# Moving 61 gathered dot products into a later part of a mixture kernel, and splitting a gate multiplication over two engines

## The chip, the cores and the metric

The kernel runs on one NeuronCore of a Trainium2 chip. The metric is device time in microseconds, the median of several runs: 3538.58 us before the change (three runs, 3538.36 to 3540.56). The engines are called TensorE (PE in the profile), VectorE (DVE), ScalarE (ACT), GpSimd (POOL) and SyncE (SP); each works through its own queue in program order.

## The reference

The program is two transformer-like blocks one after the other. Only the feed-forward of the first block, `peer_ffn`, matters here. For each of 512 tokens and 8 heads it picks 16 of 16384 experts and sums them:

```python
s1, s2 = q1 @ sub_keys_1, q2 @ sub_keys_2          # 128 scores each, per head
v1, i1 = top_k(s1, 16); v2, i2 = top_k(s2, 16)
cand = v1[:, None] + v2[None, :]                   # 16 x 16 sums
top_s, pos = top_k(cand, 16)
expert = i1 * 128 + i2 at pos                      # 16 of 128 x 128 experts
gate = softmax(top_s)
act = gelu(x . w_down[expert]) * gate              # 128 dot products a token
y = sum(act * w_up[expert])                        # 128 rows a token
```

`w_down` and `w_up` have 16384 rows of 1024 floats each (64 MB).

## The kernel before, in words

The function `phase_b` computes this in two ways at once. For the last 384 tokens (`ND` = 3 tiles of 128) it is done densely: all 128 blocks of 128 experts are scored for all tokens, the Gelu of the scores is multiplied with a gate map that is zero where a token did not choose an expert, and the product is multiplied with all of `w_up`. For the first 128 tokens (`NG` = 1 tile) the chosen rows are gathered from memory.

**Parts in time.** The code of `phase_b` is scheduled by hand: instructions stand in each engine's queue in the order in which Python issues them. There are three loops over expert blocks `b`:

1. *Score blocks*, `b` from 0 to `FUSE` - 1 = 87. `score` (L1206) takes a prepared weight, runs 24 matmuls of 128x384 into a bank `pS`, and ScalarE writes the Gelu into a stage `sst`, which goes out to memory (`smap`) every second block. Beside it runs the generator `side`: first `topk` for four tiles (VectorE: top-16 searches, comparisons, sums, a softmax whose exponential is on ScalarE at L911), then `gate_map` (L918) for three tiles.
2. *Fused blocks*, `b` from `FUSE` to 127: `score`, then `act` (L1203: VectorE multiplies score and gate into `ua`, ScalarE copies its rounded high part `uah`, VectorE subtracts for the low part `ual`), then `up_mm` for the block before: 18 matmuls of 128x512 into six banks `py`.
3. *Up blocks*, `b` from 0 to `FUSE` - 1: scores come back from `smap`, `act`, `up_mm`.

**Weights.** Each block of weights (128x1024 floats) is loaded by SP three ahead, and split two ahead (`split`, L1342): ScalarE casts the high part `wsh` (L1346), GpSimd subtracts for the low part `wsl` (L1347). A fused block needs two such splits, the others one.

**Gate maps.** `gate_map` makes, for four tokens at a time, one-hot rows of the two expert indices (L944, 128x1024, both in one comparison), multiplies the first half with the gates (L946, 128x512), and in the next step `flush` lets TensorE multiply the two one-hots (L932, bank `pgm`) and ScalarE copy the result into a stage `gst` (L933); every fourth step the stage goes to memory (`gmap`). The one-hots have two buffers, so the comparison of a step waits for the matmuls of the step two before. There are 32 steps a tile, 96 in all.

**Gathers.** `gather_tiles` (L953) has 128 down rows and 64 pairs of up rows to fetch. GpSimd issues an indirect DMA (L974) seven ahead into eight buffers; VectorE forms the dot product of a down row with the token (L984, 128x1024); up pairs are multiplied on TensorE (L1008).

**Budgets.** How much of a generator is issued in a block is set by `take(gen, budget)`: each `yield` of the generator names a cost, and steps are issued while credit is left. A top-k tile costs 35 credits, a gate-map step 1.9, a dot product 1, an up pair 2. `side` gets 3.3 a block for the first 12 blocks and `SR` after; `gat` gets `GR` in score blocks from block 12 on, `GF` in fused blocks, `GR2` in up blocks:

```python
if up is None and take(side, 3.3 if b < 12 else SR):   # L1228
    sr.close(); up = self.pool(sr, "up", side="right")
if up is not None and FUSE // 8 not in GT and b > FUSE - 8:
    load_g(FUSE // 8)                                  # on SP's queue, ahead of later weights
if b >= 12:
    take(gat, GR)
```

When `side` is done its pool is released, the pool `up` takes its room, and the first gate map is loaded back from memory.

Of the kernel before, what the change touches and what calls it, by code (L numbers as in the profile page):

```python
# [12 lines left out]
AF = mybir.ActivationFunctionType  # L13
# [78 lines left out]
    return {k: np.ascontiguousarray(v) for k, v in o.items()}  # L92


SR, GR, GR2 = 4.0, 0.8, 1.4
FUSE, GF = 88, 2.0
NG, GB = 1, 8
ND = 4 - NG
NT = 128 * ND
# [7 lines left out]
class K:  # L107
# [810 lines left out]
    def gate_map(self, pool, t, e2, gate):  # L918
        nc = self.nc
        pT = pool.tile([128, 3, 128], F32, name="gmT", bufs=1)  # L920
        p = self.bank("pgt")
        for q, src in enumerate((e2[:, 0], e2[:, 1], gate)):
            nc.tensor.transpose(p[:, q * 128:(q + 1) * 128], src.rearrange("p h k -> p (h k)"), self.ident)
        nc.scalar.copy(pT, p[:, :384].rearrange("p (q t) -> p q t", q=3))
        yield 0.0
        pend = None

        def flush(last):
            stage, q, b, oh = pend
            p = self.bank("pgm")  # L930
            for w in range(4):
                nc.tensor.matmul(p[:, w * 128:(w + 1) * 128], oh[:, 1, w], oh[:, 0, w], start=True, stop=True)  # L932
            nc.scalar.copy(stage[:, :, 4 * q:4 * q + 4].rearrange("p i t -> p t i"),  # L933
                           p.rearrange("p (t i) -> p t i", t=4))
            if q == 3:
                nc.scalar.dma_start(self.gmap[(t - NG) * 8 + b], stage.rearrange("p i t -> p (i t)"))

        for b in range(8):
            stage = pool.tile([128, 128, 16], F32, name="gst", bufs=2)
            for q in range(4):  # L940
                oh = pool.tile([128, 2, 4, 128], F32, name="oh", bufs=2)
                t0 = b * 16 + q * 4
                B4 = [128, 2, 4, 128]
                nc.vector.tensor_tensor(oh, self.io128[:, None, None, :].to_broadcast(B4),  # L944
                                        pT[:, :2, t0:t0 + 4][:, :, :, None].to_broadcast(B4), op=OP.is_equal)
                nc.vector.tensor_mul(oh[:, 0], oh[:, 0], pT[:, 2, t0:t0 + 4][:, :, None].to_broadcast([128, 4, 128]))  # L946
                yield 1.9
                if pend is not None:
                    flush(False)
                pend = (stage, q, b, oh)  # L950
        flush(True)
# [1501 lines left out]
```

## Time and profile before

| what | value |
|---|---|
| median of the runs | 3538.58 us |
| the profiled execution's own time | 3550.41 us |
| its span, first to last instruction | 3548.7 us |
| mean granted TensorE clock | 0.939 |
| busy: TensorE, VectorE, ScalarE, GpSimd | 3163.8, 2415.0, 1328.9, 1808.1 us |
| first and last score activation of `phase_b` | 677.0 and 1596.3 us |

The profiled execution is some 12 us longer than the median. A row of a timeline gives the start in us, the duration in us, the engine, the line, the operation, the tile written and the tiles read, and in brackets how long the engine stood idle before and what released it. A row of a grouping gives a count, the busy time in us and the mean in ns. Reported durations contain time in which an instruction has begun and is held back.

### The profile page before, as it was taken

Reading aid. Unit: us, or ns where it says so; the run is one execution under the profiler, and the core shown is the slowest. Engines: PE = TensorE matmul, PEld = TensorE weight load, DVE = VectorE, ACT = ScalarE, POOL = GpSimd, SP = SyncE. Lnnn points to the kernel's source line nnn. Section 1 sums busy time; section 2 is a strip of 40 time slices with the busy share of each in tenths; the row PEclk is TensorE's granted clock in tenths of the full one; section 3 lists DMA queues with packets and bytes.
Section 4 is the critical chain, followed back from the end, with each engine's and each line's share of the span. In section 5 each row is a group of like instructions: output and inputs, shape, how many; then the busy total and the mean of one; then the engine's idle time right before and its main releaser. Section 6 shows DMA issues by size and latency. Waiting matters only on the chain. (4 is left out here: it accounts for less than half of the span.)

```text
span 3548.7 us, 43925 instructions
## 1 busy us (share of the span) xinstructions
PE 3163.8 (89%) x16324; PEld 2429.7 (68%) x16324; DVE 2415.0 (68%) x3200; ACT 1328.9 (37%) x1887; POOL 1808.1 (51%) x970
## 2 busy tenths in 40 slices
PE   7777899978788899999999999877899999999995
PEld 7767798977788899876666686754455555555541
DVE  6999756999999779836666664676555455554524
ACT  3234523332455433323232334253344434444421
POOL 4656553466555489977777643233233323333313
PEclk8888899989999999999999998889999999999997
DMA  3111122355666688779989721568999999999996
GB/s 100 60 60 60 34 66 87 111 199 192 215 242 234 226 272 284 266 240 328 328 316 335 251 95 49 179 230 311 341 371 380 390 388 376 389 394 382 380 387 238
DMA packets 286347, 868.15 MB, mean 245 GB/s; under 512 B 21232, under 2 KB 82064, under 8 KB 282928
## 3 DMA queue, kind: packets, MB, share of 16 engines
q1 hardware_dynamic: 232496, 666.64, 52.3%
q0 software_dynamic: 43264, 155.02, 12.3%
q10 hardware_dynamic: 10368, 43.63, 3.2%
q8 instruction: 130, 2.13, 0.2%
q14 instruction: 89, 0.73, 0.1%
HBM read 805.89 MB, written 59.32 MB: 244 GB/s over the span
## 5 line engine op out<-in xcount | busy, mean ns | idle before, releaser
L1347 POOL TENSOR_TENSOR wsl<-wf,wsh 128x1024 fp32r<-128x1024 f32 x272 | 687.4, 2534 | 415.4 <-ACT wsh L1346 413.5
L1799 DVE TENSOR_TENSOR m_wl<-m_wf,m_wh 128x1024 fp32r<-128x1024 f32 x256 | 395.6, 1570 | 467.6 <-ACT m_wh L1797 452.8
L1799 POOL TENSOR_TENSOR m_wl<-m_wf,m_wh 128x1024 fp32r<-128x1024 f32 x128 | 326.3, 2556 | 695.7 <-ACT m_wh L1797 600.3
L1797 ACT CAST m_wh<-m_wf 128x1024 fp32r<-128x1024 f32 x384 | 383.4, 1047 | 379.0 <-issue 161.1
L1347 DVE TENSOR_TENSOR ual<-ua,uah 128x384 fp32r<-128x384 f32 x128 | 386.4, 3019 | 168.0 <-ACT uah L1346 168.0
L1346 ACT CAST wsh<-wf 128x1024 fp32r<-128x1024 f32 x272 | 285.4, 1051 | 363.1 <-POOL wsl L1347 166.9
L2202 PE MATMUL pd<-m_wf,m_xs 128*64 128x512 f32 x1632 | 393.5, 630 | 1.6 <-DMA m_wf<-in_e_down_dram 1.6
L126 PE MATMUL pS<-xh,wsl 128*128 128x384 f32 x1024 | 352.6, 344 | 25.2 <-POOL wsl L1347 25.2
L124 PE MATMUL pS<-xh,wsh 128*128 128x384 f32 x1024 | 356.8, 348 | 16.8 <-ACT wsh L1346 16.8
L125 PE MATMUL pS<-xl,wsh 128*128 128x384 f32 x1024 | 350.9, 343 | 0.0
L125 PE MATMUL pd<-m_wl,m_xh 128*128 128x512 f32 x768 | 307.3, 400 | 13.5 <-DVE m_wl L1799 13.5
L124 PE MATMUL pd<-m_wh,m_xh 128*128 128x512 f32 x768 | 314.6, 410 | 0.0
L124 PE MATMUL py<-wsh,uah 128*128 128x512 f32 x768 | 308.9, 402 | 1.0 <-ACT uah L1346 1.0
L126 PE MATMUL py<-wsh,ual 128*128 128x512 f32 x768 | 303.9, 396 | 3.1 <-DVE ual L1347 3.1
L126 PE MATMUL pd<-m_wh,m_xl 128*128 128x512 f32 x768 | 306.5, 399 | 0.0
L125 PE MATMUL py<-wsl,uah 128*128 128x512 f32 x768 | 303.5, 395 | 0.0
L2202 PEld LDWEIGHTS pd<-m_wf,m_xs 128*64 128x64 f32 x1632 | 115.0, 143 | 225.8 <-issue 214.1
L377 DVE SCALAR_TENSOR_TENSOR cvo<-glu,cv,cvo 128x512 f32<-128x512 f32 x200 | 223.6, 1158 | 1.2
L126 PEld LDWEIGHTS pS<-xh,wsl 128*128 128x128 f32 x1024 | 196.7, 192 | 30.7 <-POOL wsl L1347 29.4
L124 PEld LDWEIGHTS pS<-xh,wsh 128*128 128x128 f32 x1024 | 197.9, 193 | 25.0 <-ACT wsh L1346 17.7
L984 DVE SCALAR_TENSOR_TENSOR gu<-gu,xn 128x1024 f32<-128x1024 f32 x128 | 207.2, 1639 | 5.4 <-DMA gu<-in_w_dn_dram,idx 5.4
L974 POOL DMA_INDIRECT gu<-in_w_dn_dram,idx x128 | 182.5, 1426 | 50.2 <-DVE gu L984 28.9
(612 smaller groups left out, 6586.0 us busy)
## 6 DMA issues: line engine op xcount, KB each, us to landing
m_wf<-in_e_gate_dram SPq DMA_DIRECT2D x132, 1024.0 KB, 11.7
m_wf<-in_e_up_dram SPq DMA_DIRECT2D x132, 1024.0 KB, 11.2
m_wf<-in_e_down_dram SPq DMA_DIRECT2D x132, 1024.0 KB, 11.8
wf<-in_w_dT_dram SPq DMA_DIRECT2D x128, 512.0 KB, 4.2
wf<-in_w_up_dram SPq DMA_DIRECT2D x128, 512.0 KB, 5.6
gmap<-gst ACTq DMA_DIRECT2D x24, 1024.0 KB, 6.2
G<-gmap SPq DMA_DIRECT2D x16, 1536.0 KB, 13.3
smap<-sst ACTq DMA_DIRECT2D x44, 384.0 KB, 3.5
```

What stands on the lines that cost most here:

```text
L124: nc.tensor.matmul(ps, a[0], b[0], start=start, stop=False)
L125: nc.tensor.matmul(ps, a[0], b[1], start=False, stop=False)
L126: nc.tensor.matmul(ps, a[1], b[0], start=False, stop=stop)
L377: nc.vector.scalar_tensor_tensor(acc, glu[:, 16 + q:528 + q], self.cv[:, o + q:o + q + 1], acc, op0=OP.mult, op1=OP.add)
L974: nc.gpsimd.indirect_dma_start(out=u, out_offset=None, in_=todo[issued][0], in_offset=bass.IndirectOffsetOnAxis(ap=todo[issued][1], axis=0))
L984: nc.vector.scalar_tensor_tensor(us[0], us[0], 1.0, xn, op0=OP.mult, op1=OP.mult, accum_out=act[i][:, j:j + 1])
L1346: nc.scalar.copy(hi, src)
L1347: (lo_eng or nc.vector).tensor_tensor(lo, src, hi, op=OP.subtract)
L1797: nc.scalar.copy(wh[:, k2], w[:, k2])
L1799: eng.tensor_tensor(wl[:, k2], w[:, k2], wh[:, k2], op=OP.subtract)
L2202: nc.tensor.matmul(ps[0][c], x[:, k], wh[:, k2, ns], start=(k == 0), stop=False)
```

## The change

Three constants move and one VectorE operation is split. The gathered dot products get no budget in score blocks (`GR` 0.8 to 0.0) and more in fused and up blocks (`GF` 2.0 to 3.0, `GR2` 1.4 to 1.45). The top-k and gate-map generator gets 4.5 credits a block instead of 4.0. Fused blocks begin at 80 instead of 88. In the gate maps, VectorE multiplies the gates in for two of the four tokens, and ScalarE for the other two, as an Identity activation with a scale per partition, in place.

```diff
-SR, GR, GR2 = 4.0, 0.8, 1.4
-FUSE, GF = 88, 2.0
+SR, GR, GR2 = 4.5, 0.0, 1.45
+FUSE, GF = 80, 3.0
...
                 nc.vector.tensor_tensor(oh, self.io128[:, None, None, :].to_broadcast(B4),
                                         pT[:, :2, t0:t0 + 4][:, :, :, None].to_broadcast(B4), op=OP.is_equal)
-                nc.vector.tensor_mul(oh[:, 0], oh[:, 0], pT[:, 2, t0:t0 + 4][:, :, None].to_broadcast([128, 4, 128]))
+                nc.vector.tensor_mul(oh[:, 0, :2], oh[:, 0, :2], pT[:, 2, t0:t0 + 2][:, :, None].to_broadcast([128, 2, 128]))
+                for w in range(2, 4):
+                    nc.scalar.activation(oh[:, 0, w], oh[:, 0, w], AF.Identity, scale=pT[:, 2, t0 + w:t0 + w + 1])
                 yield 1.9
                 if pend is not None:
                     flush(False)
```

## Rows read from the trace of the kernel before

**Rows 1.** The page's first part: busy time, share of the span, instructions.

```profile
PE 3163.8 (89%) x16324; PEld 2429.7 (68%) x16324; DVE 2415.0 (68%) x3200; ACT 1328.9 (37%) x1887; POOL 1808.1 (51%) x970
```

**Rows 2.** Busy us by window: stretch, length, PE, PEld, DVE, ACT, POOL, clock, DMA.

```profile
672.00:893.90 221.90, 177.94 (x947) 173.93 (x945) 208.57 (x427) 69.78 (x91) 139.83 (x65) 0.91 0.55 184
893.90:1214.20 320.30, 284.37 (x1813) 277.45 (x1814) 300.81 (x260) 161.56 (x186) 177.41 (x82) 0.97 0.67 234
...
1251.70:1596.80 345.10, 336.45 (x1694) 296.79 (x1694) 261.68 (x215) 117.96 (x159) 299.40 (x156) 0.99 0.79 264
1596.80:2053.00 456.20, 446.71 (x2088) 311.71 (x2087) 300.57 (x216) 139.77 (x195) 329.31 (x201) 0.99 0.86 303
```

**Rows 3.** ScalarE's timeline: score activations, start and duration in us.

```profile
855.82 0.49 ACT L1212 ACTIVATE sst<-pS 128x384 f32<-128x384 f32 x1 [2.24 <-PE pS L126]
...
860.06 0.49 ACT L1212 ACTIVATE sst<-pS 128x384 f32<-128x384 f32 x1 [2.81 <-PE pS L126]
...
1014.13 0.49 ACT L1212 ACTIVATE sst<-pS 128x384 f32<-128x384 f32 x1 [2.22 <-PE pS L126]
...
1020.16 0.49 ACT L1212 ACTIVATE sst<-pS 128x384 f32<-128x384 f32 x1 [1.65 <-PE pS L126]
1020.68 0.33 ACTq L1227 DMA_DIRECT2D smap<-sst  x1
...
1548.87 0.49 ACT L1212 ACTIVATE sst<-pS 128x384 f32<-128x384 f32 x1 [7.17 <-PE pS L126]
...
1558.35 0.49 ACT L1212 ACTIVATE sst<-pS 128x384 f32<-128x384 f32 x1 [4.27 <-PE pS L126]
```

**Rows 4.** VectorE's timeline in the fused part, one block.

```profile
1303.79 4.97 DVE L1347 TENSOR_TENSOR ual<-ua,uah 128x384 fp32r<-128x384 f32 x1 [0.58 <-ACT uah L1346]
1308.69 1.21 DVE L984 SCALAR_TENSOR_TENSOR gu<-gu,xn 128x1024 f32<-128x1024 f32 x1
...
1309.84 1.21 DVE L984 SCALAR_TENSOR_TENSOR gu<-gu,xn 128x1024 f32<-128x1024 f32 x1
...
1310.98 0.55 DVE L1200 TENSOR_TENSOR ua<-sst,G 128x384 f32<-128x384 f32 x1
1312.11 4.97 DVE L1347 TENSOR_TENSOR ual<-ua,uah 128x384 fp32r<-128x384 f32 x1 [0.58 <-ACT uah L1346]
```

**Rows 5.** GpSimd's timeline beside it.

```profile
1303.56 4.78 POOL L1347 TENSOR_TENSOR wsl<-wf,wsh 128x1024 fp32r<-128x1024 f32 x2
1308.50 1.10 POOL L974 DMA_INDIRECT gu<-in_w_dn_dram,idx  x1 [0.16 <-issue]
1309.91 1.96 POOL L974 DMA_INDIRECT gu<-in_w_dn_dram,idx  x1 [0.30 <-DVE gu L984]
```

**Rows 6.** GpSimd's timeline where the gathers begin: two of seven issues.

```profile
739.13 0.94 POOL L974 DMA_INDIRECT gu<-in_w_dn_dram,idx  x1 [0.30 <-issue]
740.37 0.94 POOL L974 DMA_INDIRECT gu<-in_w_dn_dram,idx  x1 [0.30 <-issue]
```

**Rows 7.** The dot products' line alone (L984), by window; a read of the accumulator each.

```profile
672.00:893.90 221.90, 51.59 (x42) 0.91 0.55 184
```

**Rows 8.** ScalarE's timeline: the last of four top-k exponentials.

```profile
890.81 0.31 ACT L911 ACTIVATE gate<-gate 128x128 f32<-128x128 f32 x1 [16.24 <-DVE gate L910]
```

**Rows 9.** The gate multiplication: its group from 893 to 1221 us, one unhindered.

```profile
L946 DVE TENSOR_TENSOR oh<-oh,gmT 128x512 f32<-128x512 f32 x96 | 136.8, 1425 | 3.3
...
1007.96 0.69 DVE L946 TENSOR_TENSOR oh<-oh,gmT 128x512 f32<-128x512 f32 x1
```

**Rows 10.** ScalarE's groups from 672 to 2060 us, shapes apart.

```profile
L933 ACT COPY gst<-pgm 128x512 f32<-128x512 f32 x96 | 100.9, 1071 | 63.2 <-PE pgm L932 62.8 <-ACT gst L933 0.5
...
L993 ACT COPY aT<-pgt 128x128 f32<-128x128 f32 x1 | 0.3, 266 | 0.9 <-PE pgt L991 0.9
```

**Rows 11.** All instructions of L1448, an Identity activation after L1488's Gelu.

```profile
L1448 ACT ACTIVATE c_qT<-pq,c_bq x5: 688/690/690, 2103.3 to 2125.1; 128x512 f32<-128x512 f32 x5
```

**Rows 12.** ScalarE's timeline after the last gate map.

```profile
1237.35 1.04 ACT L1346 CAST wsh<-wf 128x1024 fp32r<-128x1024 f32 x1 [11.88 <-DMA wf<-in_w_dT_dram]
```

## The prediction, as it was made before the result was known

> **What bounds the kernel now.** I read the page's busy shares first [rows 1], then the windows by part [rows 2], then the timelines of single engines inside the parts. The reader sees in [rows 1] that TensorE is busy for 89% of the span, so VectorE's work only counts where TensorE waits for it. [rows 2] shows where. In the first two parts (top-k, then gate maps) VectorE is busy 209 of 222 us and 301 of 320 us; in the fused part (scores and up products together) and in the up part TensorE is busy 336 of 345 us and 447 of 456 us. So the first 542 us are VectorE's, and everything from 1251.7 us on is TensorE's.
>
> TensorE's own pace comes from consecutive score activations [rows 3]. A bare score block takes 4.24 us (860.06 less 855.82). A block with two gate-map steps and no dot product takes 6.03 us (1020.16 less 1014.13), so one step's matmuls cost (6.03 - 4.24) / 2 = 0.90 us. A fused block takes 8.32 us (VectorE's `ual` comes at 1303.79 and 1312.11, [rows 4]), of which the up product is 8.32 - 4.24 = 4.08 us. With one gathered up pair it takes 9.48 us (1558.35 less 1548.87), so a pair is 1.16 us.
>
> The rows to look at longest are VectorE's in the fused part [rows 4] beside GpSimd's [rows 5]. The two hold each other out: `ual`, a 0.55 us subtraction, lasts 4.97 us, because GpSimd's two weight subtractions (4.78 us together) run in that time. GpSimd's loop is full as well: 0.16 gap + 1.10 first gather issue + 0.30 gap + 1.96 second issue + 4.78 = 8.30 us. The second issue ends 0.82 us after the dot product it lay beside (1309.84 + 1.21 = 1311.05, end 1311.87); with VectorE waiting an issue takes 0.94 us, 1.24 us from the next [rows 6]. So at two dot products a block three engines stand at 8.3 us, and VectorE and GpSimd have nothing left.
>
> **The change part by part.**
>
> *The order of the work, counted from the budgets.* The top-k and gate-map generators cost 140 + 182.4 credits. Before, the gate maps run from block 37 to 82; after, with 4.5 a block, from 34 to 74, with 4.5 / 1.9 = 2.37 steps a block instead of 2.11. Before, 61 of the 128 dot products fall into the first part and 67 into the fused part, two a block. After, none falls into the first part and all 128 into the fused part, three a block: 42.7 of its 48 blocks. There are 8 fewer score-only blocks, 8 more fused ones, 8 fewer up-only ones. TensorE's total work stays as it was; only its waiting changes.
>
> *Top-k part (35 blocks after, 38 before).* VectorE is busy 208.6 us [rows 2], 51.6 us of it in dot products [rows 7], of which 21 x 1.21 = 25 us is their work and 26 us waiting for GpSimd. ScalarE stands behind VectorE here (16.24 us at one exponential, [rows 8], four such places), which holds weight casts back. Without the dot products VectorE needs 157 us, and it was idle for 13. If all their waiting goes, the part takes 157 (TensorE's floor, 35 x 4.24 = 148, lies under it); if the waiting merely falls on other two-input operations, 222 - 27 = 195. I take 175, nearer the first, since most top-k operations that remain keep their usual duration beside the weight subtraction: -47 us.
>
> *Gate maps.* The multiply of 128x512 had a mean of 1.43 us, but 0.69 unhindered [rows 9]; half of it is about 0.35. Two ScalarE multiplications of 128x128 come in its place: the trace has 0.27 for a copy of that shape [rows 10] and 0.31 for an exponential [rows 8], so about 0.6 us a step, 55 us of ScalarE in all. ScalarE has the room (162 of 320 us busy), but not the place: the multiplications of a step stand in its queue behind the block's Gelu (0.49 us) and, every second block, the store's issue (0.33 us, [rows 3]). TensorE wants that step's one-hots 0.90 us after the scores end; ScalarE delivers them at about 0.04 + 0.49 + 0.6 = 1.1, or 1.5 with the issue. That is a new wait of about 0.5 us, and in a block with three steps, where the third multiplication also stands behind a 1.07 us eviction [rows 10], about 1.3. Behind it wait the evictions, the weight cast, and GpSimd's subtraction for it. TensorE's floor is 40.3 x 4.24 + 96 x 0.90 = 257 us; the waits add 25.4 x 0.5 + 14.9 x 1.3 = 32, the stray stalls of such a part 6. I take 295, with bounds 262 (no new wait) and 310: -25 us. Identity should cost no table: five activations with it follow a tanh-Gelu without a load [rows 11]. Were there loads after all, they would lie in ScalarE's queue at the same place, which rival D prices.
>
> *The stretch from the last gate map to the fused part.* It holds five blocks in both kernels and the same hole (ScalarE waits 11.88 us for weights, [rows 12], whose loads stand in SP's queue behind the gate map's load, which waits for the released pool): 37.5 us, unchanged.
>
> *Fused part.* The gathers start only here, so seven issues go out at once, 6 x 1.24 + 0.94 = 8.4 us of GpSimd ahead of a weight subtraction; with two weights prepared ahead I put 4 us of that on TensorE (0 to 8). Then three dot products a block. At the least, if VectorE and GpSimd only keep each other's tensor operations out, a block needs 3 x 1.15 (their spacing in [rows 4]) + 0.55 + 0.55 + 4.78 = 9.33 us. VectorE's loop as it stands, with one dot product more, is 8.32 + 1.15 = 9.47. GpSimd's loop with a third issue is 8.30 + 0.30 + 0.94 = 9.54, or 10.56 if that issue too is held by a dot product for 1.96. I take 10.0, between these, and keep 9.3 and 10.6. Total: 4 + 42.7 x 10.0 + 5.3 x 8.32 + 8 pairs x 1.16 + 7 for the turn from dot products to up rows (ScalarE waits 7.17 us for the scores that end before 1548.87, [rows 3]) = 491; before 345: +146 us. Gathers themselves have room: DMA is busy 79% here [rows 2], and a longer block lowers it.
>
> *Up part.* 8 x 4.08 + 1.16 less: -34 us. The slightly larger budget moves nothing: all pairs are issued inside it in both kernels.
>
> *Sum.* -47 - 25 + 146 - 34 = +40 us against the profiled execution's span of 3548.7 (3550.4 with what lies around it). That execution is 12 us above the median of the runs, so the forecast for the median is 3538.6 + 40 = 3579.
>
> *A rule of the Trainium skill.* The 1.96 us issue beside a dot product [rows 5] against 0.94 alone [rows 6] says that a two-input VectorE operation holds a gather issue back. The Trainium skill, "SBUF — State Buffer", section "Who interferes with whom", has it otherwise: such an operation contends with what GpSimd reads, not with its descriptor generation (which the page marks as inferred). By the rows a block is 10.0 and the sum +40; by the page issues stay short, and the lock on the tensor operations alone is left, which is rival B.
>
> **The rivals.**
>
> *B: only the tensor operations exclude each other; gather issues are not held.* GpSimd's loop is then 4.78 + 0.16 + 3 x 0.94 + 0.60 = 8.36, VectorE and GpSimd together 9.33, fused part 463 us: +12, 3551 us. For it: a first issue takes 1.10 although a dot product starts in it. Against it: the steady 1.96 of every second issue.
>
> *C, not slower: the whole of VectorE's relief reaches TensorE.* Place: the first two parts. ScalarE's multiplications arrive in time (VectorE, freed, runs a step ahead), and the exponentials no longer find VectorE behind. The parts go to 157 and 262 us, -65 and -58: with the fused part as forecast that is -123 + 146 - 34 = -11, 3528 us; with rival B's fused part -39, 3500. It decides from the point where the first two parts together give 112 us. For it: VectorE's 94% in both. Against it: ScalarE's in-order queue, and that TensorE waits in the gate maps now only 320 - 45 x 4.24 - 96 x 0.90 = 43 us.
>
> *D: worse.* The third issue always held and a wait added by it (10.6), ScalarE's place costing more (310), the top-k waits staying (195): -27 - 10 + 172 - 34 = +101, 3640 us.
>
> That the change does not do what it says can be set aside: with a budget of 0.0 no credit comes up before block 80.
>
> **How the numbers follow.** Forecast 0.50, B 0.15, C 0.22, D 0.13. The bounds for faster and slower are 0.2%, 7 us. The forecast gives 0.03 faster, 0.02 same, 0.45 slower; B 0.03, 0.03, 0.09; C 0.18, 0.03, 0.01; D all slower. Together faster 0.24, same 0.08, slower 0.68. The forecast's own range is 3549 (9.3 a block) to 3604 (10.6). The whole range takes in B, more than half of C and a part of D: 3510 to 3625.
>
> **What would show it.** Right: dot products only after block 80, three a block; score activations there 9.5 to 10.6 us apart, TensorE waiting for `wsl` in that part; issues of nearly 2 us, three a block; the first part shorter by some 70 us, with `pgm` waiting for ScalarE's `oh`. Wrong: fused blocks under 9.1 us (the sum changes sign there: 40 / 42.7 = 0.9 less than forecast), a dot product running while a weight subtraction runs, gate-map blocks near 6.4 us, or table loads beside Identity.

## The result, and the profile after

The changed kernel takes 3586.71 us (median of 4 runs, 3583.53 to 3588.86); on the same chip the kernel before takes 3539.57 (3538.36 to 3542.55). The ratio is 1.0131, interval 1.0114 to 1.0149: slower, near the forecast of 3579. The profiled execution has a span of 3586.8 us and took 3588.56, so it lies 1.9 us above its median, while the one of before (3550.41) lies 10.8 above the 3539.57; the spans differ by 38.1 us and the medians by 47.1.

The page's busy shares of the changed kernel, for [rows 1]:

```profile
PE 3179.2 (89%) x16324; PEld 2443.5 (68%) x16324; DVE 2359.2 (66%) x3200; ACT 1386.6 (39%) x2079; POOL 1786.5 (50%) x970
```

They hardly moved. VectorE works 56 us less and ScalarE 58 us more, and the kernel is slower: the page's first part can't say where. The windows by part, in the columns of [rows 2], can:

```profile
666.40:842.60 176.20, 159.74 (x875) 158.10 (x873) 169.02 (x381) 64.04 (x84) 103.05 (x35) 0.95 0.43 143
842.60:1157.00 314.40, 271.52 (x1698) 268.75 (x1699) 194.54 (x194) 212.86 (x369) 97.42 (x40) 0.93 0.47 164
...
1190.50:1664.30 473.80, 415.42 (x2038) 360.01 (x2038) 389.53 (x353) 142.05 (x192) 416.37 (x241) 0.98 0.87 287
```

In the first part VectorE still fills 169 of 176 us, but there is less of it. In the gate maps VectorE fell from 301 to 195 us busy and the stretch became only 6 us shorter: nobody is full there now, so something waits. In the fused part TensorE, 98% busy before, is busy 415 of 474 us.

The same cuts in both kernels, by the starts of the first one-hot comparison (L944), the last, the last score activation ahead of the fused blocks, and the last of all (us; the last columns are experiments told below):

| part | before | changed | difference | forecast | e3 | e6 | e10 |
|---|---|---|---|---|---|---|---|
| start to first scores | 677.0 | 671.4 | -5.6 | 0 | 672.7 | 672.8 | 667.7 |
| top-k | 217.8 | 172.1 | -45.6 | -47 | 171.9 | 172.4 | 171.9 |
| gate maps | 321.4 | 312.8 | -8.6 | -25 | 252.8 | 312.7 | 253.0 |
| to the fused part | 35.1 | 33.7 | -1.4 | 0 | 40.9 | 33.7 | 41.0 |
| fused part | 345.1 | 473.8 | +128.7 | +146 | 481.2 | 406.4 | 409.2 |
| up part and the rest | 1952.4 | 1923.0 | -29.4 | -34 | 1922.1 | 1919.1 | 1919.4 |
| span | 3548.7 | 3586.8 | +38.1 | +40 | 3541.6 | 3517.1 | 3462.1 |

The signs are as forecast; the gate maps gave a third of what was put on them. The first row varies between 667.7 and 677.0 us among the kernels of this case, although none of the edits touches that stretch, so a few us in one row of one profile show nothing.

**The fused block.** VectorE's timeline in the changed kernel, for [rows 4] (start, duration, instruction, idle time ahead of it):

```profile
1315.70 4.95 DVE L1349 TENSOR_TENSOR ual<-ua,uah 128x384 fp32r<-128x384 f32 x1 [0.58 <-ACT uah L1348]
1320.57 1.21 DVE L986 SCALAR_TENSOR_TENSOR gu<-gu,xn 128x1024 f32<-128x1024 f32 x1
...
1321.72 1.22 DVE L986 SCALAR_TENSOR_TENSOR gu<-gu,xn 128x1024 f32<-128x1024 f32 x1
...
1324.01 0.62 DVE L1202 TENSOR_TENSOR ua<-sst,G 128x384 f32<-128x384 f32 x1
1325.21 4.96 DVE L1349 TENSOR_TENSOR ual<-ua,uah 128x384 fp32r<-128x384 f32 x1 [0.58 <-ACT uah L1348]
```

GpSimd's beside it, for [rows 5]:

```profile
1315.47 4.75 POOL L1349 TENSOR_TENSOR wsl<-wf,wsh 128x1024 fp32r<-128x1024 f32 x2
1320.38 1.10 POOL L976 DMA_INDIRECT gu<-in_w_dn_dram,idx  x1 [0.16 <-issue]
1321.79 1.95 POOL L976 DMA_INDIRECT gu<-in_w_dn_dram,idx  x1 [0.30 <-issue]
1324.04 0.94 POOL L976 DMA_INDIRECT gu<-in_w_dn_dram,idx  x1 [0.30 <-issue]
1325.00 4.74 POOL L1349 TENSOR_TENSOR wsl<-wf,wsh 128x1024 fp32r<-128x1024 f32 x2
```

And TensorE's wait for the low part of a weight, with two score activations of ScalarE, for [rows 3]:

```profile
1312.54 0.49 ACT L1214 ACTIVATE sst<-pS 128x384 f32<-128x384 f32 x1 [4.55 <-PE pS L126]
1317.93 0.44 PE L126 MATMUL pS<-xh,wsl 128*128 128x384 f32 x1 [0.95 <-POOL wsl L1349]
1322.08 0.49 ACT L1214 ACTIVATE sst<-pS 128x384 f32<-128x384 f32 x1 [4.32 <-PE pS L126]
```

From weight subtraction to weight subtraction GpSimd takes 1325.00 - 1315.47 = 9.53 us, and the score activations follow at 9.54. GpSimd has no gaps here but those of 0.16 and 0.30 us ahead of its issues, so its loop is the block. One issue in three is held to 1.95 us; the third runs in 0.94, because VectorE is then at the short `ua`. In 16 of 128 cases that one is held too, to 1.32, until 0.8 us after `ua`, and the block takes 9.9. Over blocks 84 to 121 the mean is (1593.49 - 1236.14) / 37 = 9.66 us. By the view of waits from 1236 to 1593 us, TensorE and its weight load stand here:

```profile
PEld pS L126 <- POOL wsl L1349: 51.9, 37, 1.7
...
PE pS L126 <- POOL wsl L1349: 40.1, 37, 1.4
```

One wait a block, and 51.9 / 37 = 1.40 us is what the block has grown by (9.66 less 8.28, TensorE's own pace, which e6 shows below). (The weight load waits along with TensorE; the two rows are one wait, not to be added.)

The part's opening is dearer. Nine gather issues go out between 1194.6 and 1206.1 us, and the weight subtraction behind them comes late; TensorE waits 6.12 us for it, and 3.14 us for the next:

```profile
1208.89 0.69 PE L126 MATMUL pS<-xh,wsl 128*128 128x384 f32 x1 [6.12 <-POOL wsl L1349]
```

**A gate-map block with three steps.** One of 15, the engines in order of time:

```profile
916.07 1.95 PE L932 MATMUL pgm<-oh 128*128 128x128 f32 x16
916.35 0.48 ACT L1214 ACTIVATE sst<-pS 128x384 f32<-128x384 f32 x1
916.52 2.36 POOL L1349 TENSOR_TENSOR wsl<-wf,wsh 128x1024 fp32r<-128x1024 f32 x1 [4.43 <-ACT wsh L1348]
917.16 2.79 DVE L944 TENSOR_TENSOR oh<-io,gmT 128x1024 f32<-128x1024 f32 x1 [1.94 <-PE pgm L932]
919.99 0.43 DVE L946 TENSOR_TENSOR oh<-oh,gmT 128x256 f32<-128x256 f32 x1
919.99 0.69 ACT L948 ACTIVATE oh<-oh,gmT 128x128 f32<-128x128 f32 x2 [1.79 <-DVE oh L944]
920.56 1.13 PE L932 MATMUL pgm<-oh 128*128 128x128 f32 x8 [2.54 <-DVE oh L946]
```

There are two one-hot buffers. TensorE uses both at 916.07 to 918.0, and VectorE may write the third step's one-hots only when TensorE has read the first: VectorE waits 1.94 us for `pgm`. Then its comparison, 1.22 us elsewhere, takes 2.79 because a weight subtraction has just begun, then come the gates, and TensorE has waited 2.54 us, by the profile for VectorE's half of the one-hots; ScalarE's half is done at about the same time. That isn't all the block pays. Four windows of 1 us behind it (the third number from the end is the granted clock):

```profile
921.00:922.00 1.00, 1.00 (x10) 1.00 (x9) 0.97 (x3) 1.00 (x3) 0.00 (x0) 0.98 0.53 213
922.00:923.00 1.00, 1.00 (x5) 1.00 (x4) 1.00 (x2) 1.00 (x2) 0.00 (x0) 0.50 0.00 0
...
925.00:926.00 1.00, 1.00 (x6) 1.00 (x6) 0.00 (x0) 0.26 (x1) 0.66 (x1) 0.81 1.07 434
926.00:927.00 1.00, 1.00 (x8) 1.00 (x7) 0.00 (x0) 0.00 (x0) 1.00 (x1) 1.00 0.54 221
```

TensorE resumes, and from 921.9 to 925.3 us it runs at 1.2 GHz instead of 2.4, which costs (3 x 0.50) + 0.19 = 1.7 us more. The block takes 4.24 + 3 x 0.90 + 2.54 + 1.7 = 11.2; measured from activation to activation it is 927.49 - 916.35 = 11.14. Two-step blocks mostly take 6.03, TensorE's own pace. The view of waits from 843 to 1157 us puts it together:

```profile
DVE oh L944 <- PE pgm L932: 105.1, 40, 4.8
...
PE pgm L932 <- DVE oh L946: 45.6, 17, 5.4
PEld pgm L932 <- issue: 40.1, 15, 3.2
```

All of TensorE's waits end with VectorE's `oh` (L946); none is put down to ScalarE's multiplications (L948). The two rows of 45.6 and 40.1 us are largely the same waits, of the matmuls and of their weight load.

Read in windows of 1 us, the part begins at the lower clock and has 10 further falls, and the shortfall (1 less the granted clock, over all windows under 0.9) adds up to 20.4 us, of which 17.0 lie in the 10; in the part of before it is 7.8. The length of the wait alone doesn't decide on a fall. Ten of the 15 blocks, with waits of 2.19 to 3.00 us, had one and took 10.4 to 11.2 us; the other five, with waits of 1.54, 1.74, 1.79, but also 2.46 and 3.02, had none and took 8.9 to 9.6. What decides was not tried.

### The profile page after: what moved, and what is told of

Same layout as the page of the kernel before. It is cut to its first block, busy times and chain, and to the rows that moved or that the text cites. A ratio compares the mean times of both kernels' runs of the same rounds, so it can differ in the third digit from the quotient of the medians.

```text
span 3586.8 us, 44026 instructions
## 1 busy us (share of the span) xinstructions
PE 3179.2 (89%) x16324; PEld 2443.5 (68%) x16324; DVE 2359.2 (66%) x3200; ACT 1386.6 (39%) x2079; POOL 1786.5 (50%) x970
## 5 line engine op out<-in xcount | busy, mean ns | idle before, releaser
L1349 POOL TENSOR_TENSOR wsl<-wf,wsh 128x1024 fp32r<-128x1024 f32 x272 | 673.6, 2486 | 495.1 <-ACT wsh L1348 464.7
L1349 DVE TENSOR_TENSOR ual<-ua,uah 128x384 fp32r<-128x384 f32 x128 | 418.6, 3271 | 166.4 <-ACT uah L1348 166.3
L126 PE MATMUL pS<-xh,wsl 128*128 128x384 f32 x1024 | 360.2, 352 | 59.1 <-POOL wsl L1349 59.1
L944 DVE TENSOR_TENSOR oh<-io,gmT 128x1024 f32<-128x1024 f32 x96 | 147.7, 1539 | 116.4 <-PE pgm L932 105.1
L125 PEld LDWEIGHTS pS<-xl,wsh 128*128 128x128 f32 x1024 | 201.6, 197 | 1.8
```

Of the source, the lines that this page charges most:

```text
L125: nc.tensor.matmul(ps, a[0], b[1], start=False, stop=False)
L126: nc.tensor.matmul(ps, a[1], b[0], start=False, stop=stop)
L1349: (lo_eng or nc.vector).tensor_tensor(lo, src, hi, op=OP.subtract)
```

## The experiments

Two questions: what sets the fused block (the theory: VectorE and GpSimd exclude each other and one gather issue is held; the rivals: one of the two alone, or neither), and where VectorE's relief in the gate maps went. Every ratio below is to runs of the kernel before on the same chip. The changed kernel ran on one chip only, so differences from its 3586.71 us are taken between chips (the kernel before has medians of 3539.57 to 3543.52 us on them) and are good to some 4 us.

**e1: one input instead of two.**

```diff
-nc.vector.scalar_tensor_tensor(us[0], us[0], 1.0, xn, op0=OP.mult, op1=OP.mult,
-                               accum_out=act[i][:, j:j + 1])
+nc.vector.tensor_reduce(act[i][:, j:j+1], us[0], axis=AX.X, op=OP.add)
```

> The changed kernel, but each gathered dot product (two inputs: the row and the token) becomes a sum of the gathered row (one input, the same 1024 elements); the multiplication with the token is left out. Gathers, issues, counts and order stay. Theory (VectorE's two-input operations and GpSimd's weight subtractions and gather issues hold each other out): fused blocks fall from 9.5-9.9 us to 8.3-8.5, issues no longer last 1.95 us, the kernel gets 45 us shorter, near 3540 us. Rival (VectorE's time for 128 operations of 1.2 us is what fills the block): blocks stay at 9.5, time stays at 3587 within 10 us. Rival (the gathers' issues or their transfers set the pace): the same, no change.

Measured: 3558.32 us (3552.61 to 3563.55), ratio 1.0044 (1.0026 to 1.0061); mean block (1566.29 - 1226.28) / 37 = 9.19. VectorE and GpSimd, one timeline each:

```profile
1326.10 3.46 DVE L986 TENSOR_REDUCE act<-gu 128x1 f32<-128x1024 f32 x3
1329.48 2.88 DVE L1201 TENSOR_TENSOR ua<-sst,G 128x384 f32<-128x384 f32 x1
```

```profile
1327.32 0.94 POOL L976 DMA_INDIRECT gu<-in_w_dn_dram,idx  x1 [0.30 <-DVE act L986]
1328.56 0.94 POOL L976 DMA_INDIRECT gu<-in_w_dn_dram,idx  x1 [0.31 <-DVE act L986]
1329.53 2.42 POOL L1348 TENSOR_TENSOR wsl<-wf,wsh 128x1024 fp32r<-128x1024 f32 x1
1333.94 2.40 POOL L1348 TENSOR_TENSOR wsl<-wf,wsh 128x1024 fp32r<-128x1024 f32 x1 [2.00 <-ACT wsh L1347]
```

Beside a sum with one input the issues take 0.94 (mean 0.98 over all 128): it is the two-input operation that holds them. The edit also takes away that operation's output of 128x1024, so the second input and the write are not told apart. But the block came to 9.19 and not 8.5. Two of three blocks do take 8.5; in the third (10.4) the lock works in another place. `ua` begins beside a weight subtraction and lasts 2.88 us; ScalarE's `uah` and the weight cast stand behind it, and GpSimd idles 2.00 us for that cast. So the held issue is not the whole.

**e2: no gather issues on GpSimd.** The rows fetched are consecutive ones, not the gathered ones.

```diff
+if issued < 128:
+    nc.sync.dma_start(u, A["w_dn"][issued * 128:(issued + 1) * 128])
+else:
     nc.gpsimd.indirect_dma_start(out=u, out_offset=None, in_=todo[issued][0],
...
```

> The changed kernel, but the 128 rows of a gather are loaded by SyncE as 128 consecutive rows instead of an indirect DMA on GpSimd (so the choice of rows is left out); the dot products stay. Theory (the lock on tensor operations is the larger part: 3 x 1.15 + 0.55 + 0.55 + 4.78 = 9.33): fused blocks stay at 9.3-9.5 us, 0 to 15 us off the kernel. Rival (GpSimd's three issues, 1.10 + 1.95 + 0.94 with gaps, set the pace): GpSimd has only 4.78 us of work in a block, which falls to 8.3 us, 45 to 55 us off the kernel.

Measured: 3559.53 us (3557.07 to 3561.99), ratio 1.0045 (1.0028 to 1.0061); mean block 9.26. VectorE:

```profile
1320.82 0.56 DVE L1352 TENSOR_TENSOR ual<-ua,uah 128x384 fp32r<-128x384 f32 x1 [0.58 <-ACT uah L1351]
1321.30 1.22 DVE L989 SCALAR_TENSOR_TENSOR gu<-gu,xn 128x1024 f32<-128x1024 f32 x1
1322.44 3.40 DVE L989 SCALAR_TENSOR_TENSOR gu<-gu,xn 128x1024 f32<-128x1024 f32 x1
1325.77 3.41 DVE L989 SCALAR_TENSOR_TENSOR gu<-gu,xn 128x1024 f32<-128x1024 f32 x1
1330.24 0.56 DVE L1352 TENSOR_TENSOR ual<-ua,uah 128x384 fp32r<-128x384 f32 x1 [0.58 <-ACT uah L1351]
```

The loop of VectorE is 9.42 us without a single issue on GpSimd: two of three dot products wait out a weight subtraction. That is the 9.33 of the lock alone, within 0.1. Six of eight loops take 9.4; in the other two ScalarE waits up to 3.9 us for a weight, whose load now shares SyncE's queue with the rows, and they take 7.2 to 8.3 and about 11, so the mean is no clean figure of the lock. The changed kernel's 9.66 is 0.2 us above 9.43, which is the most that the issues add on top. Two limits lie side by side, VectorE with the subtractions at 9.4 and GpSimd's loop at 9.5: taking one away leaves the other.

**e7: short dot products** (over the first 64 of 1024 elements).

```diff
-nc.vector.scalar_tensor_tensor(us[0], us[0], 1.0, xn, op0=OP.mult, op1=OP.mult,
+nc.vector.scalar_tensor_tensor(us[0][:, :64], us[0][:, :64], 1.0, xn[:, :64], op0=OP.mult, op1=OP.mult,
```

> The changed kernel with dot products over the first 64 of 1024 elements (the rest is left out); gathers, issues and order stay. The row sums took 0.47 of the extra 1.34 us a block away and left VectorE its time; here the time goes too. Theory (VectorE's time and the lock together): blocks of 8.3-8.5 us, 45 to 55 us off. Rival (three gather issues beside two subtractions fill GpSimd by themselves): blocks stay above 9.

Measured: 3533.29 us (10 runs, 3525.28 to 3540.09), ratio 0.9976 (0.9964 to 0.9988); blocks 8.5 (one of 9.7). With VectorE's share gone the fused part is nearly TensorE's again, though not quite (8.28, below): three issues (1.10, 0.94 and 0.94), two subtractions and the gaps make 8.5 us of GpSimd by themselves.

**e5 and e6: one, or both, weight subtractions of a fused block on VectorE.**

```diff
-HL[i] = self.split(bp, W.pop(i), [128, 1024], "ws", bufs=3, lo_eng=nc.gpsimd)
+fused = 16 + FUSE < i <= 16 + FUSE + 2 * (128 - FUSE)
+eng = nc.vector if fused and (i - 16 - FUSE) % 2 == 0 else nc.gpsimd    # e5
+eng = nc.vector if fused else nc.gpsimd                                 # e6
+HL[i] = self.split(bp, W.pop(i), [128, 1024], "ws", bufs=3, lo_eng=eng)
```

> The changed kernel; in the fused blocks the low part of the up weights (one of the two GpSimd subtractions of a block) is formed by VectorE. Theory (the block is the sum of what VectorE and GpSimd must do apart from each other): VectorE's two-input work 4.55 + 1.2 = 5.75 and GpSimd's 2.39 make 8.1 us instead of 9.3, below TensorE's 8.32, so blocks go to 8.3-8.8 us and the kernel gets 35 to 55 us shorter. Rival (VectorE's own time is what counts, since it was never idle but for 0.58 us a block): 1.2 us more work on it makes blocks 10.9 us, 50 us longer.

> The changed kernel; in the fused blocks VectorE forms the low part of both weights, GpSimd only issues gathers. Theory: nothing of GpSimd's is left to hold VectorE out; VectorE has 4.55 + 2.4 + 0.58 = 7.5 us a block, so TensorE sets 8.3-8.5 us, 45 to 57 us off. It may fall short if the score weights' subtraction, which now stands in VectorE's queue behind the dot products, comes late. Rival (VectorE's own time): blocks of 12 us, 100 us longer.

Measured: e5 3542.05 us (10 runs), ratio 1.0009 (0.9997 to 1.0021), blocks 8.84 and 8.88; e6 3518.23 us (3511.66 to 3519.86), ratio 0.9931 (0.9915 to 0.9948), blocks 8.29. VectorE in e6:

```profile
1437.08 1.23 DVE L1350 TENSOR_TENSOR wsl<-wf,wsh 128x1024 fp32r<-128x1024 f32 x1 [0.40 <-ACT wsh L1349]
1438.22 1.22 DVE L986 SCALAR_TENSOR_TENSOR gu<-gu,xn 128x1024 f32<-128x1024 f32 x1
...
1442.80 0.56 DVE L1203 TENSOR_TENSOR ua<-sst,G 128x384 f32<-128x384 f32 x1
1443.93 0.56 DVE L1350 TENSOR_TENSOR ual<-ua,uah 128x384 fp32r<-128x384 f32 x1 [0.58 <-ACT uah L1349]
```

A subtraction of 1.22 us is one that took GpSimd some 2.4 (4.75 for two), `ual` is back at 0.56 in all 48 blocks, and no dot product is held any more. The rival of both runs, blocks of 10.9 or 12 us by VectorE's own time, fell. VectorE's loop, 5 x 1.15 + 2 x 0.56 and its fixed gaps, fits into TensorE's 8.29. So the engine that was said to be full had room for two more operations a block, because about half of what filled it (4.4 of 9.0 us a block) was waiting for the other engine. e6 lies 69 us under the changed kernel, 12 to 24 more than I had expected: the fused part alone gave 67 of them (table): 51 from the 37 blocks, 12 from the opening, where no subtraction stands behind the first issues any more, and most of the rest from the turn to the up rows.

**e3: six one-hot buffers instead of two**, in what the top-k's `big` tiles occupy.

```diff
-big = lambda: bpool.tile([128, 2048], F32, name="big", bufs=2)
+big = lambda: bpool.tile([128, 2048], F32, name="big", bufs=3)
...
-oh = pool.tile([128, 2, 4, 128], F32, name="oh", bufs=2)
+if q % 2 == 0:
+    pair = pool.tile([128, 2048], F32, name="big", bufs=3).rearrange("p (s a w f) -> p s a w f", s=2, a=2, w=4)
+oh = pair[:, q % 2]
```

> The changed kernel with six one-hot buffers in the gate maps instead of two (three tiles of the top-k scratch hold two each). Theory (the third step of a block waits for a buffer: comparison after the first step's matmuls, then gates, then matmuls): the blocks with three steps fall from 11.1 us to about 7.0, 15 of them, 50 to 65 us off the gate-map part and the kernel, near 3530 us. Rival (my prediction: the ScalarE multiplications stand late in ScalarE's queue): the wait stays, less than 10 us off.

Measured: 3540.88 us (10 runs, 3532.63 to 3554.23), ratio 0.9998 (0.9983 to 1.0013); three-step blocks 7.2 to 7.9 us (one of them 927.22 - 920.07 = 7.15). The whole gate-map part by window:

```profile
844.60:1097.50 252.90, 246.56 (x1632) 243.57 (x1633) 214.65 (x192) 196.26 (x354) 102.04 (x38) 0.99 0.56 198
```

TensorE is busy 247 of 253 us, at a granted clock of 0.99 instead of 0.93. The part is 60 us shorter than in the changed kernel; its clock shortfall is 2.6 us instead of 20.4, so some 18 of the 60 are the clock and some 42 the waits themselves. Part of it is given back: the fused part is 7 us longer (blocks of 9.9; why more of them was not tried), the stretch before it 7 (table). With buffers enough, the wait for ScalarE's half of the gates comes into sight, and it is small (843 to 1113 us: total, count, longest):

```profile
PE pgm L932 <- ACT big L950: 4.7, 8, 0.8
```

**e4: the gates wholly on VectorE again**, in the changed kernel.

```diff
-nc.vector.tensor_mul(oh[:, 0, :2], oh[:, 0, :2], pT[:, 2, t0:t0 + 2][:, :, None].to_broadcast([128, 2, 128]))
-for w in range(2, 4):
-    nc.scalar.activation(oh[:, 0, w], oh[:, 0, w], AF.Identity, scale=pT[:, 2, t0 + w:t0 + w + 1])
+nc.vector.tensor_mul(oh[:, 0], oh[:, 0], pT[:, 2, t0:t0 + 4][:, :, None].to_broadcast([128, 4, 128]))
```

> The changed kernel with the gate multiplication whole on VectorE again (the budgets and the fused start as changed). Theory (in this part VectorE has time to spare, it waited 105 us for matmuls, and what counts is the length of the chain comparison, gates, matmuls): the chain goes from 1.22 + 0.43 + 0.70 to 1.22 + 0.69, so three-step blocks get 0.4 us shorter and the kernel stays within 10 us of 3587. Rival (the split relieves the bound engine): 96 x 0.27 = 26 us more.

Measured: 3566.05 us (3559.80 to 3568.65), ratio 1.0067 (1.0050 to 1.0083); three-step blocks mostly 8.3 to 8.4 instead of 8.9 to 11.2. ScalarE's weight cast, GpSimd's subtraction, VectorE's third comparison and TensorE at one of them:

```profile
1018.17 1.07 ACT L1346 CAST wsh<-wf 128x1024 fp32r<-128x1024 f32 x1
1019.32 2.42 POOL L1347 TENSOR_TENSOR wsl<-wf,wsh 128x1024 fp32r<-128x1024 f32 x1 [2.90 <-ACT wsh L1346]
1021.29 2.27 PE L932 MATMUL pgm<-oh 128*128 128x128 f32 x16
1022.38 1.23 DVE L944 TENSOR_TENSOR oh<-io,gmT 128x1024 f32<-128x1024 f32 x1
1024.47 1.13 PE L932 MATMUL pgm<-oh 128*128 128x128 f32 x8 [0.92 <-DVE oh L946]
```

The expectation, within 10 us of the changed kernel, fell: it gained 21. By the length of the chain (one multiplication of 0.69 against 0.43 and 0.70 on two engines side by side) the split costs nothing. What it costs is a place in ScalarE's queue, and by these rows through the weight cast: without the multiplications ahead of it the cast, and the subtraction behind it, come earlier (the subtraction starts 3.1 us ahead of the third comparison, in the changed kernel's block 0.6), and it is over when the comparison begins. None of the 96 comparisons lasts longer than 1.23 us here; in the changed kernel 18 last over 2. So 1.6 of the 2.54 us of wait were VectorE held out by GpSimd once more. Here the wait is 0.92 and the clock stays at 1.00 in all windows around it; over the part the shortfall is 5.8 us instead of 20.4. The part is 27 us shorter (285.6 against 312.8), of which the clock would be 15; the fused part gives 10 back.

**e8: the kernel before with the split alone** (the edit of the diff at L946, the budgets as before).

```diff
-nc.vector.tensor_mul(oh[:, 0], oh[:, 0], pT[:, 2, t0:t0 + 4][:, :, None].to_broadcast([128, 4, 128]))
+nc.vector.tensor_mul(oh[:, 0, :2], oh[:, 0, :2], pT[:, 2, t0:t0 + 2][:, :, None].to_broadcast([128, 2, 128]))
+for w in range(2, 4):
+    nc.scalar.activation(oh[:, 0, w], oh[:, 0, w], AF.Identity, scale=pT[:, 2, t0 + w:t0 + w + 1])
```

> The kernel before with only the gate multiplication split over VectorE and ScalarE (old budgets, fused from 88). Moving it back gave the changed kernel 25 us. Theory (the ScalarE half lengthens the chain from comparison to matmuls, which counts where a block has three steps: 15 blocks after, 5 before; elsewhere VectorE is the bound here and loses 0.27 us a step): between 20 us shorter and 5 us longer. Rival (ScalarE's place in the queue costs in every step): 25 us longer.

Measured: 3524.58 us (6 runs, 3518.48 to 3532.65), ratio 0.9960 (0.9947 to 0.9972). Most blocks stand 6.43 us apart (6.8 to 7.0 before), and the gate-map part goes from 321 to 301 us. VectorE waits only 16.0 us for `pgm` from 900 to 1180 us (105.1 in the changed kernel), so it is VectorE that has less to do. The same edit is worth -14 us where VectorE sets the pace and, by e4, +21 in the changed kernel, where its dot products are gone already.

**e9: the third step taken out of the budgets.**

```diff
-SR, GR, GR2 = 4.5, 0.0, 1.45
-FUSE, GF = 80, 3.0
+SR, GR, GR2 = 4.0, 0.0, 1.65
+FUSE, GF = 88, 3.0
```

> The changed kernel with the old 4.0 credits a score block and the old fused start at 88 (so two gate-map steps a block, rarely three); the split and the dot products after the score blocks stay (three in each of the 40 fused blocks, the last 8 in the up part with 1.65 credits a block). Theory (4.5 credits bring a third step into every third block, and the third step costs 5 us): gate-map blocks at 6.0-6.5 us, four or five of 11, the kernel 30 to 45 us shorter than the changed one, near 3550. Rival (the number of steps a block does not matter, the same 96 steps wait the same): within 10 us of 3587.

Measured: 3542.15 us (10 runs, 3534.51 to 3546.52), ratio 0.9990 (0.9975 to 1.0004). Gate-map blocks are mostly 6.03, a few with three steps 8.7 to 10.3; the fused ones stay at 9.5 to 9.9. With few third steps the move of the dot products costs nothing on the whole: against the kernel before, the fused part loses 44 us and the up part, which now has the last 8 dot products and the turn to the up rows, 24; the top-k gives 42 and the gate maps 27. The edit moves the budgets and the fused start together, so it doesn't single out the third step; e3 and e4 do.

**e10: e6 and e3 together.**

> The changed kernel with both causes taken away: VectorE forms the low parts in the fused blocks, and the gate maps have six one-hot buffers. Theory (two separate waits of TensorE, 68 us and 50 us, which add up): 3518 - 50 = 3468 us, 2% under the kernel before. Rival (a shared bound takes over, DMA or the top-k part's end): 3490 to 3518.

Measured: 3464.30 us (5 runs, 3463.03 to 3469.89), ratio 0.9786 (0.9767 to 0.9806): faster than both kernels, by 2.1% than the one before. The gate maps and the fused part by window:

```profile
839.50:1092.60 253.10, 246.89 (x1632) 243.90 (x1633) 212.53 (x192) 196.32 (x354) 101.88 (x38) 0.99 0.55 198
1133.60:1542.70 409.10, 403.90 (x2038) 360.73 (x2037) 310.59 (x446) 142.30 (x191) 219.04 (x145) 0.99 0.95 337
```

TensorE is busy 98% in the one and 99% in the other. The gains add: -46 (e3) and -69 (e6) make -115, measured -122. In the fused part DMA's mean share is 0.95 now (0.87 in the changed kernel), and its blocks take 8.37, not 8.29; whether the transfers make that difference was not tried.

## Why the prediction was right

- *Top-k, -47.* Measured -46. The rest of VectorE's work kept its durations, as assumed, with one exception: the product at L898 (128x2048, two inputs) went from a mean of 2.81 to 4.11 us, 10.5 us in all, so part of the dot products' waiting passed to it.
- *Gate maps, -25.* The step that failed. Measured -9; the part came to 313, just outside the upper bound of 310. A wait for ScalarE's half of the gates was put at 0.5 us in every two-step block and 1.3 in a three-step one, 32 us in all. By the view of waits TensorE waited for that half nowhere in the changed kernel, and 4.7 us in all in e3. In most two-step blocks there is no wait (6.03); in the block shown there are 2.54 + 1.7 us, over the 15 three-step blocks a mean of 2.5 us of wait and 1.1 of lower clock. I had ScalarE's place in the queue as the cause, and e4 shows it as a part, by another way than I thought: it shifts the weight subtraction onto the third comparison. Left out were the buffers (with two, a third step can't start before the first is read: e3 takes nearly the whole wait away), the lock on that comparison, and the clock that falls after ten of these waits.
- *Fused part, +146.* Measured +129. Mechanism right, sizes off both ways. I had put the third issue between held and free; it is mostly free, and the block takes 9.66, not 10.0: some 14 us less. The sum counted 48 intervals with an up product; the first two hold none (4.16 and 4.17 us, as in the kernel before): 12 less. The opening cost 10 us, not 4 (nine issues, not seven): 6 more. The turn and the blocks behind it came to 70, not 67: 3 more. The lock's bound of 9.33 is what e2 shows without issues (9.4), and the GpSimd loop of 9.54 what the changed kernel shows with them. That DMA would be less busy in longer blocks was wrong: its mean share went from 0.79 to 0.87, with three rows a block in place of two; from 1236 to 1593 us no wait of VectorE for a gathered row shows.
- *Up part, -34, and the turn.* Measured -29, the stretch after the up part included; the turn lies in the fused part, as in the sum.
- *Identity without a table load.* Right; as before, ScalarE's Gelu and Identity follow each other with no load between them.
- The two wrong sizes, +16 in the gate maps and -17 in the fused part, cancel by luck, so the sum of +40 against the span (+38) is better than its terms. The median came out 8 us above the forecast because the two profiled executions lie differently to their medians (10.8 and 1.9 above), and a sum of spans was laid on a median.
- *Rival B (issues not held)* fell: the second issue is held at 1.95, and 0.94 beside a sum with one input (e1). The Trainium skill, "SBUF — State Buffer", section "Who interferes with whom", says that a two-input VectorE operation contends with what GpSimd reads, and infers that descriptor generation is spared. Here the dot product does hold the issue, to 0.8 us after its own end. But a gather's issue reads its indices too (`idx` in its rows), and no run tells that read from the descriptors, so the rows contradict the inference only if the read is not what waits. What that section of the Trainium skill says of a one-input reduction, that it doesn't contend, e1 bears out for the issues. *Rival C* needed 112 us from the first two parts; they gave 54. In e3 they give 46 + 69 = 115, and the time is that of before: its condition was a matter of buffers (six instead of two), though its own price of -11 was not quite reached (span -7, the medians alike). *Rival D* did not come about, though its gate-map part did (310).

## What to carry to other kernels

A busy share says nothing of room where two engines lock each other out: price an operation on VectorE by its unhindered duration, and ask whether the other engine's work can be moved so that the lock ends (4.95 us of `ual` became 0.56). Before more steps are put into a unit of work, count the buffers between producer and consumer: with two, the third step is a round trip through both engines' queues, and TensorE pays for the wait and, in ten of 15 blocks here, again for the clock after it.

## What the runs showed of the hardware

- A wait of 2.54 us was followed, 1.3 us after TensorE had resumed, by 3.4 us at 1.2 GHz: 1.7 us on top. Ten of 15 such waits (1.54 to 3.02 us) in the gate maps had such a fall behind them, five had none, among them the longest. In e4 a wait of 0.92, with one shorter hole before it, was followed by none.
- A gather issue took 0.94 us alone [rows 6] and beside a one-input sum (e1), and 1.95 beside a dot product of 1.22 with two inputs; GpSimd was held, the dot product not.
- Two GpSimd subtractions in a row (4.75 us) held a VectorE subtraction of 0.56 us for 4.95: VectorE did not get in between them.
- An Identity activation of 128x128 with a scale for each partition took 0.69 us for two; the half multiplication on VectorE 0.43, more than half of the whole one's 0.69 [rows 9].
